# Half-array products chained to alternate, the values' projection behind the first scores, and an order chosen with short queues

## The chip, the cores and the metric

The kernel runs on one core of a Trainium2 chip. The profile names the core's engines: PE multiplies matrices (PEld loads its weights beside it), ACT, DVE and POOL work elementwise, and SP issues the weight transfers. The metric is the time of one execution on the device in microseconds (us), given as the median of several runs. The profile and the trace come from one execution, whose own time stands in the table below.

## The reference

A network of twelve residual sub-layers over 256 tokens of width 1024. Every sub-layer normalizes its input, computes, and is added to the residual stream.

```python
for layer in range(2):                      # first block
    y = even_mixer(...) if layer % 2 == 0 else diff_mixer(...)
    x = x + rms_norm(y, g[1])
    y = memory_cross_attention(rms_norm(x, g[2]), mem_n, ...)
    x = x + rms_norm(y, g[3])
    x = x + rms_norm(swiglu(rms_norm(x, g[4]), ...), g[5])
for l in range(2):                          # second block
    x = x + 0.5 * swiglu_2(rms_norm_2(x, ffn1_norm[l]), ...)
    # neighbourhood attention, gated linear attention (gla), latent attention (mla)
    mixed = gt0 * (y_na @ w_br_na) + gt1 * (y_gla @ w_br_gla) + gt2 * (y_mla @ w_br_mla)
    x = x + mixed @ w_out[l]
    x = x + 0.5 * swiglu_2(rms_norm_2(x, ffn2_norm[l]), ...)
```

`even_mixer` holds two attentions of 8 heads of 64 (`fox_attention`, causal with a bias from forget gates, and `nsa_attention`, the sum of a compressed, a selected and a window branch). `diff_mixer` subtracts one softmax from another. The matrix products of an attention are, for every head,

```python
s = einsum('bqhd,bkhd->bhqk', q, k) * scale      # scores: contraction over the 64 of a head
p = masked_softmax(s, mask)
o = einsum('bhqk,bkhd->bqhd', p, v)              # weighing: 64 results for a query
```

## The kernel before

The twelve stages run in the order even, mem0, ffn0, odd, mem1, ffn1, then f10, mix0, f20, f11, mix1, f21. The 256 tokens are two tiles `t` of 128. Weights are streamed once, in pieces of 512 KB, by the SP queue into four raw buffers (`fetch`, L361). Each piece is split into a high and a low part, the high one by ACT (L386) and the low one by DVE (L388), and a projection adds three products of such parts (L395 to L397, or L403 to L406). Transposes run on PE as well (L451).

The products of attention are in plain f32, and one such product is two instructions in the trace. A head has 64 features, half the height or the width of PE's array of 128 by 128. Scores (`score_unit`, L686) contract over 64 rows: head `h` of a pair uses the row half `h`, and the two halves write to two banks of PSUM, `S[0]` and `S[1]`. A score unit is one tile `t` and two or four pairs of heads; its two banks go through a softmax each (ACT and DVE), are transposed and copied to `PT`, and are then weighed. Weighing (`weigh` L702, and L868 and L872 in `nsa_attention`) has 64 result columns: head `h` uses the column half `h`, and both halves write to one bank `O`. The rotary part of mla (L1311) and the updates and scores of gla (L1397, L1419) work by row halves too. In this text a **piece** is a run of half-array instructions that stand next to each other in PE's order, and the trace writes their shape as `64*128` (row half) or `128*64` (column half).

The order of the instructions on each engine is not the order of the code. The Tile framework's scheduler picks, in a simulation of the time line, what each engine does next, and each engine then runs its list strictly in order. Two things bind the scheduler: data dependences, and `after` (L231), an edge that says that an instruction stands behind another one on its engine. Weights run ahead of their use as far as buffers allow, so projections of the same or the next matrix are there to fill PE while a softmax runs. In `even` and in both halves of `odd` the projection of the values `V` is written ahead of the loop over score units.

At the end of the odd stage the last weighed bank is copied by ACT (`xnA`, L443) and normalized by DVE (`tokA`, L983), then transposed by PE, and the output projection uses it. The same engines split the pieces of the weights that follow, `od_out` and then `memq` of the next stage.

Of the kernel before, what the change touches and what calls it, by code (L numbers as in the profile page):

```python
# [12 lines left out]

F32 = mybir.dt.float32
# [9 lines left out]
KT = 8  # L24
# [177 lines left out]
class Net:  # L202
# [27 lines left out]
    @contextmanager  # L230
    def after(self, *instructions):  # L231

        with ExitStack() as order:
            for i in instructions:
                order.enter_context(self.tc.issue_after(i))
            yield

    def point(self, act, dve):

# [435 lines left out]
    def score_unit(self, unit, qT, kT, extra=None, mask=True):  # L675


        mm = self.nc.tensor.matmul
        t, w, prs = unit
        n = len(prs)  # L680
        S = [self.bank("s")[:, :n * w].rearrange("p (n w) -> p n w", w=w) for _ in range(2)]
        q = slice(t * 128, (t + 1) * 128)
        for i, p in enumerate(prs):
            for h in range(2):
                r = slice(h * 64, h * 64 + 64)
                mm(S[h][:, i], qT[r, p, q], kT(p)[r, :w], start=i == 0 or not mask, stop=not mask)  # L686
        for h in range(2):
            if extra:
                for i in range(0, n, 2):
                    extra(S[h][:, i:i + 2], prs[i] + h, w)  # L690
            if mask:
                mm(S[h][:, :, w - 128:], self.identb, self.causal[:, None, :].to_broadcast([128, n, 128]), start=False,
                   stop=True)
        return S

    def weigh(self, O, V, PTs, prs, nb, c0=0):

        for i, p in enumerate(prs):
            for h in range(2):
                for b in range(nb):  # L700
                    c = c0 + p * 128 + h * 64
                    self.nc.tensor.matmul(O[h * 64:h * 64 + 64, p], V[:, b, c:c + 64], PTs[h][:, i * nb + b], start=b == 0,  # L702
                                          stop=b == nb - 1)


    def rope_consts(self):
# [81 lines left out]
    def even(self, xT, finish, filler):  # L788
        nc = self.nc
        mm = nc.tensor.matmul  # L790
        self.mode("ring")
        st = self.stream("ev_in")
        hd = lambda a: a.rearrange("p (h d) -> p h d", d=64)
        kT, kT2 = self.q4(8), self.u(9)[:, :512].rearrange("p (b n) -> p b n", b=2)

        kk = [self.u(2)[:, t * 416:(t + 1) * 416] for t in range(2)]
        v5 = self.u(1)[:, :768].rearrange("p (t n) -> p t n", t=2)
# [11 lines left out]
        with self.chain():  # L809
# [24 lines left out]
            for t in range(2):  # L834
# [17 lines left out]
                for u in self.causal_units():  # L852
                    if u[0] != t:
                        continue
                    w, prs = u[1:]
                    PTs = [[], []]
                    for br in range(2):
                        for h, S in enumerate(self.score_unit(u, qT2, lambda p: kT2[:, br])):
                            P, r = self.softmax(S)
                            r2 = self.sm(r.shape[-1])  # L860
                            c = 8 + 8 * br + 2 * prs[0] + h
                            nc.vector.tensor_mul(r2, r, gt[:, t, c:c + 2 * len(prs) - 1:2])
                            self.scaled(P, r2)
                            PTs[br].append(self.probsT(self.flat(P)))
                    for i, p in enumerate(prs):
                        for h in range(2):
                            o = O[h * 64:h * 64 + 64, p]
                            mm(o, self.vcbd[:, 2 * p + h], PcT[:, 0], start=True, stop=False)  # L868
                            for br in range(2):
                                for b in range(t + 1):  # L870
                                    c = 128 + br * 128 + h * 64
                                    mm(o, v5[:, b, c:c + 64], PTs[br][h][:, i * (t + 1) + b], start=False,  # L872
                                       stop=br == 1 and b == t)
                s = slice(t * 128, (t + 1) * 128)
                self.split(oT[0][:, 4:8, s], oT[1][:, 4:8, s], O)

# [94 lines left out]
    def odd(self, xT, finish, filler):  # L971
# [14 lines left out]
        for half in range(2):  # L986
# [11 lines left out]
            self.proj(st, xT, KT, (512, lambda t, ps: self.evac(V[:, t], ps)))  # L998
            with self.chain():
                for i, u in enumerate(self.causal_units()):  # L1000
                    t, w, prs = u
                    n = len(prs)
                    S1, S2 = self.score_unit(u, qT, lambda p: kT[:, p])
                    (P1, r1), (P2, r) = self.softmax(S1), self.softmax(S2)
                    r2 = self.sm(n)
                    nc.vector.tensor_scalar(r2, r, self.lamc, None, op0=ALU.mult)
# [292 lines left out]
    def mla(self, qnT, qrT, knT, krT, V):  # L1299
# [3 lines left out]
        for t in range(2):  # L1303
# [5 lines left out]
            for p, h in heads:  # L1309
                r = slice(h * 64, h * 64 + 64)  # L1310
                mm(S[h][:, p], qrT[r, p, tq(t)], krT[r, p], start=False, stop=p == 1)  # L1311
            PTs = self.probs(S)
            for p, h in heads:
                for b in range(2):
# [38 lines left out]
    def gla(self, ls, qk, V, sr, keT):  # L1353
# [20 lines left out]
        for t in range(2):  # L1374
# [5 lines left out]
            for i in range(3):  # L1380
# [9 lines left out]
                else:  # L1390

                    U = [self.bank("o").rearrange("p (h v) -> p h v", h=4) for _ in range(2)]
                    for h in range(4):
                        hs = slice(h * 128, h * 128 + 128)
                        for c in range(2):
                            r = slice(c * 64, c * 64 + 64)
                            mm(U[c][:, h], E[r, hs], V[r, t, hs], start=True, stop=True)  # L1397
# [14 lines left out]
        for t in range(2):  # L1412
            A = self.tile([128, 4, 128], F32, "PT")
            As.append(A)
            parts = [self.bank("s").rearrange("p (h i) -> p h i", h=4) for _ in range(2)]
            for h in range(4):
                for e in range(2):
                    r = slice(e * 64, e * 64 + 64)
                    mm(parts[e][:, h], keT[r, h, tq(t)], qeT[r, h, tq(t)], start=True, stop=True)  # L1419
# [96 lines left out]
        Net(ctx, tc, ins, out).run(stages or STAGES)  # L1516


# [9 lines left out]
```

## Time and profile before

| what | value |
|---|---|
| time, median of 3 runs | 2102.23 us (2100.59 to 2104.03) |
| profiled execution, own time | 2100.82 us |
| span of its trace | 2099.1 us |
| mean granted clock of PE | 0.994 |
| PE busy | 2036.3 us, 97% |
| DVE, ACT, POOL busy | 1389.0, 1168.3 and 88.6 us |

A busy share is time in which an engine's instructions run, and PE's instructions overlap, so the step from one start to the next start is the price of an instruction while nothing waits. In a time line the bracket at the end of a row is idle time before it and what ended that.

### The profile page before, as it was taken

What the parts mean: (1) busy time and instruction counts of PE and PEld (TensorE: products, weight loads), DVE (VectorE), ACT (ScalarE), POOL (GpSimd) and SP (SyncE); (2) the same over time, 40 slices, a digit from 0 to 9 for tenths busy, and PEclk for the clock granted to TensorE, in tenths of its full rate; (3) what the DMA queues carried; (4) which work ended last, traced back from release to release, by engine and by line L of the source; (5) the groups of instructions that cost most, each with busy time, mean ns of one, the idle gap of its engine ahead of it and who ended that gap; (6) DMA issues with size and microseconds to landing.
All of it is one profiled execution on the core that took longest, in us unless ns stands there. A gap on an engine that the chain in (4) does not pass through costs nothing.

```text
span 2099.1 us, 31060 instructions
## 1 busy us (share of the span) xinstructions
PE 2036.3 (97%) x11244; PEld 1707.1 (81%) x11244; DVE 1389.0 (66%) x2878; ACT 1168.3 (56%) x2547; POOL 88.6 (4%) x173
## 2 busy tenths in 40 slices
PE   7998899999799999999999999999999999999999
PEld 6876788877688889887777888888888777879887
DVE  7756765577676657565758777666664667877663
ACT  6645665455566556554654556555654555556652
POOL 1000000000100000001100000000000100100000
PEclk9999999999999999999999999999999999999999
DMA  7505476433457546553443566554653443556750
GB/s 237 176 18 188 161 231 189 145 132 120 161 170 239 184 147 219 196 181 107 148 157 119 168 201 233 190 190 150 227 188 117 149 151 116 181 171 206 235 182 31
DMA packets 100474, 352.16 MB, mean 168 GB/s; under 512 B 12468, under 2 KB 12980, under 8 KB 100320
## 3 DMA queue, kind: packets, MB, share of 16 engines
q1 hardware_dynamic: 96912, 337.99, 49.1%
q0 software_dynamic: 3408, 12.20, 1.9%
q8 instruction: 88, 1.44, 0.3%
q14 instruction: 66, 0.54, 0.1%
HBM read 349.09 MB, written 1.05 MB: 167 GB/s over the span
## 4 chain that ended last, share of the span: by engine, by line
PE 89%; DVE 5%; DMA 2%; ACT 2%; issue 1%; POOL 0%; SPq 0%; ACTq 0%; DVEq 0%; POOLq 0%
PE ps_a L395 10%; PE ps_a L397 10%; PE ps_a L396 10%; PE ps_s L406 8%; PE ps_s L404 5%; PE ps_o L395 4%; PE ps_o L397 4%; PE ps_o L396 4%; PE ps_u L406 4%; PE ps_t L406 4%; PE ps_u L404 2%; PE ps_t L404 2%; PE ps_s L397 2%; PE ps_s L395 2%; PE ps_s L396 2%; PE ps_s L686 2%
## 5 line engine op out<-in xcount | busy, mean ns | idle before, releaser
L388 DVE TENSOR_TENSOR ring<-raw,ring 128x512 fp32r<-128x512 f32 x724 | 467.3, 680 | 179.3 <-ACT ring L386 172.6
L386 ACT ACTIVATE ring<-raw 128x512 fp32r<-128x512 f32 x724 | 411.9, 617 | 189.8 <-PE ps_a L397 64.5
L388 DVE TENSOR_TENSOR slot<-raw,slot 128x512 fp32r<-128x512 f32 x548 | 355.7, 686 | 187.0 <-ACT slot L386 185.1
L386 ACT ACTIVATE slot<-raw 128x512 fp32r<-128x512 f32 x548 | 314.4, 622 | 168.4 <-PE ps_o L397 108.1
L395 PE MATMUL ps_a<-ring,XX 128*128 128x512 f32 (+3 forms) x560 | 216.6, 390 | 6.0 <-ACT XX L386 4.7
L397 PE MATMUL ps_a<-ring,XX 128*128 128x512 f32 (+3 forms) x560 | 216.6, 387 | 0.2 <-DVE XX L388 0.2
L396 PE MATMUL ps_a<-ring,XX 128*128 128x512 f32 (+3 forms) x560 | 214.7, 384 | 0.1
L406 PE MATMUL ps_s<-XX,slot 128*128 128x512 f32 x492 | 178.1, 393 | 0.0
L404 PE MATMUL ps_s<-XX,slot 128*128 128x256 f32 x552 | 145.6, 281 | 0.0
L395 PEld LDWEIGHTS ps_a<-ring,XX 128*128 128x128 f32 x560 | 105.9, 189 | 29.5 <-ACT XX L386 6.7
L397 PEld LDWEIGHTS ps_a<-ring,XX 128*128 128x128 f32 x560 | 105.9, 189 | 23.1 <-issue 3.9
L396 PEld LDWEIGHTS ps_a<-ring,XX 128*128 128x128 f32 x560 | 106.1, 189 | 19.1 <-DVE ring L388 0.8
L404 PEld LDWEIGHTS ps_s<-XX,slot 128*128 128x128 f32 x552 | 103.7, 188 | 6.8
L406 PEld LDWEIGHTS ps_s<-XX,slot 128*128 128x128 f32 x492 | 92.4, 188 | 18.7
L406 PE MATMUL ps_s<-XX,ring 128*128 128x512 f32 x264 | 96.2, 393 | 0.0
L406 PE MATMUL ps_t<-XX,slot 128*128 128x512 f32 x258 | 93.3, 393 | 0.0
L428 POOL TENSOR_TENSOR sm<-sm,mhalf 128x1 f32<-128x1 f32 (+2 forms) x72 | 60.7, 844 | 676.7 <-DVE sm L425 394.6
L395 PE MATMUL ps_s<-slot,XX 128*128 128x256 f32 x288 | 81.9, 285 | 3.8 <-ACT XX L386 3.0
L406 PE MATMUL ps_u<-XX,slot 128*128 128x512 f32 x234 | 84.2, 393 | 0.0
L397 PE MATMUL ps_s<-slot,XX 128*128 128x256 f32 x288 | 81.9, 288 | 0.1
L396 PE MATMUL ps_s<-slot,XX 128*128 128x256 f32 x288 | 81.0, 282 | 0.0
L404 PE MATMUL ps_s<-XX,ring 128*128 128x256 f32 x312 | 79.8, 281 | 0.0
(436 smaller groups left out, 4645.0 us busy)
## 6 DMA issues: line engine op xcount, KB each, us to landing
raw<-f SPq DMA_DIRECT2D x264, 512.0 KB, 4.4
raw<-ffn SPq DMA_DIRECT2D x132, 512.0 KB, 4.3
raw<-win SPq DMA_DIRECT2D x52, 512.0 KB, 4.2
raw<-wgt SPq DMA_DIRECT2D x48, 512.0 KB, 4.1
raw<-od_in SPq DMA_DIRECT2D x24, 512.0 KB, 3.9
raw<-wbr SPq DMA_DIRECT2D x24, 512.0 KB, 4.2
raw<-ev_in SPq DMA_DIRECT2D x16, 512.0 KB, 4.3
raw<-wout SPq DMA_DIRECT2D x16, 512.0 KB, 3.8
```

The costliest lines, as they stand in the source:

```text
L386: a = nc.scalar.activation(hi, src, AF.Copy, scale=scale)
L388: b = nc.vector.tensor_tensor(lo, src, hi.bitcast(F32), op=ALU.subtract)
L395: mm(out, a[0], b[0], start=first, stop=False)
L396: mm(out, a[0], b[1], start=False, stop=False)
L397: mm(out, a[1], b[0], start=False, stop=last)
L404: mm(out[:, :256], w[1], self.XX[:, k, 0], start=False, stop=False)
L406: mm(out, w[0], self.XX[:, k], start=False, stop=last)
L428: self.pow = nc.gpsimd.tensor_tensor(r, v, self.mhalf[:, :n], op=ALU.pow).ins
L686: mm(S[h][:, i], qT[r, p, q], kT(p)[r, :w], start=i == 0 or not mask, stop=not mask)
```

## The change

There are three parts. `burst` issues a list of products with an `after` edge from each to the next, so that they stand in that order on PE, though other instructions may stand between them. Scores, weighing, the rotary part of mla and two loops of gla use it with the halves taken alternately (second half first, except in mla). In `even` and `odd` the projection of `V` is called behind the first score unit's products. And `late_choice` lowers the number of instructions that the scheduler's simulation lets queue at an engine, to 6 for PE and 3 for ACT, DVE and POOL (35 and 12 in the setting before).

```diff
+    def burst(self, products):
+        last = ()
+        for out, a, b, start, stop in products:
+            with self.after(*last):
+                last = (self.nc.tensor.matmul(out, a, b, start=start, stop=stop).ins,)
...
-        for i, p in enumerate(prs):
-            for h in range(2):
-                r = slice(h * 64, h * 64 + 64)
-                mm(S[h][:, i], qT[r, p, q], kT(p)[r, :w], start=i == 0 or not mask, stop=not mask)
+        rows = (slice(0, 64), slice(64, 128))
+        self.burst((S[h][:, i], qT[rows[h], p, q], kT(p)[rows[h], :w], i == 0 or not mask, not mask)
+                   for i, p in enumerate(prs) for h in (1, 0))
...
-    def weigh(self, O, V, PTs, prs, nb, c0=0):
-        for i, p in enumerate(prs):
-            for h in range(2):
-                for b in range(nb):
-                    c = c0 + p * 128 + h * 64
-                    self.nc.tensor.matmul(O[h * 64:h * 64 + 64, p], V[:, b, c:c + 64], PTs[h][:, i * nb + b], start=b == 0,
-                                          stop=b == nb - 1)
+    def weigh(self, O, V, PTs, prs, nb):
+        self.burst((O[h * 64:h * 64 + 64, p], V[:, b, p * 128 + h * 64:p * 128 + h * 64 + 64], PTs[h][:, i * nb + b],
+                    b == 0, b == nb - 1) for i, p in enumerate(prs) for b in range(nb) for h in (1, 0))
...
+                        products += [(o[h], self.vcbd[:, 2 * p + h], PcT[:, 0], True, False) for h in (1, 0)]
+                        for br in range(2):
+                            for b in range(t + 1):
+                                for h in (1, 0):
...
+                    self.burst(products)
...
-        self.proj(st, xT, KT, (512, lambda t, ps: self.evac(V[:, t], ps)))
...
-            for u in self.causal_units():
+            for i, u in enumerate(self.causal_units()):
                 t, w, prs = u
-                PTs = self.probs(self.score_unit(u, qT, lambda p: kT[:, p], bias))
+                S = self.score_unit(u, qT, lambda p: kT[:, p], bias)
+                if i == 0:
+                    self.proj(st, xT, KT, (512, lambda t, ps: self.evac(V[:, t], ps)))
+                PTs = self.probs(S)
...
+            self.burst((S[h][:, p], qrT[rows[h], p, tq(t)], krT[rows[h], p], False, p == 1) for p, h in heads)
...
+    spec.ENG_ISSUE_QUEUE_DEPTH = {**queues, E.PE: 6, E.Activation: 3, E.DVE: 3, E.Pool: 3}
...
-    with tile.TileContext(nc, schedule_with_timeline_sim=True) as tc:
+    with late_choice(), tile.TileContext(nc, schedule_with_timeline_sim=True) as tc:
```

The same edit as in `even` stands in `odd`, and gla's two loops become bursts as mla's does.

The order of SP stays as it was, apart from names, and so does nearly all of POOL's. PE, ACT and DVE are reordered everywhere. Three places show how.

The first is on PE, in the neighbourhood attention of mix0. `ps_o_9963` is the bank that is weighed into, `PT_9989` and `PT_10010` are the transposed probabilities of the two halves, `ps_s_10079` and `ps_s_10080` are the two banks of the next score unit. Before:

```order
L702 MATMUL ps_o_9963<-PT_9989,slot_9604 64x128 x2
L686 MATMUL ps_s_10079<-slot_9608,slot_9604 128x256 x2
L451 MATMUL ps_t_10005<-identf,P_9991 128x128 x4
L702 MATMUL ps_o_9963<-PT_10010,slot_9604 64x128 x2
L702 MATMUL ps_o_9963<-PT_9989,slot_9604 64x128 x2
L702 MATMUL ps_o_9963<-PT_10010,slot_9604 64x128 x2
```

Of the changed kernel:

```order
L244 MATMUL ps_o_9963<-PT_10010,slot_9604 64x128
L244 MATMUL ps_o_9963<-PT_9989,slot_9604 64x128
L244 MATMUL ps_o_9963<-PT_10010,slot_9604 64x128
L244 MATMUL ps_o_9963<-PT_9989,slot_9604 64x128
L244 MATMUL ps_o_9963<-PT_10010,slot_9604 64x128
L244 MATMUL ps_o_9963<-PT_9989,slot_9604 64x128
L244 MATMUL ps_o_9963<-PT_10010,slot_9604 64x128
L244 MATMUL ps_o_9963<-PT_9989,slot_9604 64x128
L244 MATMUL ps_s_10079<-slot_9608,slot_9604 128x256
L459 MATMUL ps_t_10040<-identf,P_10026 128x128 x4
L244 MATMUL ps_s_10080<-slot_9608,slot_9604 128x256
L244 MATMUL ps_s_10079<-slot_9608,slot_9604 128x256
```

The weighing of a unit, which stood in two pieces of one half and then three blocks, is now one piece whose halves alternate, and the score unit's products, which stood two of one half together, are interleaved with the other bank's.

The second is on PE, in a score unit of the window branch in the even stage. `ps_s_887` and `ps_s_886` (before: `ps_s_932`) are its banks, `ps_a_...` is a projection's bank, `causal` is the mask. Before:

```order
L451 MATMUL ps_t_805<-identf,P_789 128x128 x4
L686 MATMUL ps_s_887<-slot_195,slot_191 128x256 x2
L692 LDWEIGHTS identb
L692 MATMUL ps_s_887<-causal,identb 128x2x128
L395 MATMUL ps_a_1699<-ring_1666,slot_199 128x512
L396 MATMUL ps_a_1699<-ring_1666,slot_199 128x512
L397 MATMUL ps_a_1699<-ring_1666,slot_199 128x512
L686 MATMUL ps_s_932<-slot_195,slot_191 128x256 x2
```

Of the changed kernel:

```order
L244 MATMUL ps_s_887<-slot_195,slot_191 128x256
L403 MATMUL ps_a_1450<-ring_1398,XX 128x512
L404 MATMUL ps_a_1450<-ring_1398,XX 128x512
L405 MATMUL ps_a_1450<-ring_1398,XX 128x512
L403 MATMUL ps_a_1450<-ring_1405,XX 128x512
L404 MATMUL ps_a_1450<-ring_1405,XX 128x512
L459 MATMUL ps_t_828<-identf,P_812 128x128 x4
L244 MATMUL ps_s_886<-slot_195,slot_191 128x256
L244 MATMUL ps_s_887<-slot_195,slot_191 128x256
L244 MATMUL ps_s_886<-slot_195,slot_191 128x256
```

A bank that had its two products and its mask in one go now gets its first product alone, with projection products and transposes behind it, and its second one between the products of the other bank.

The third is on ACT, at the end of the odd stage. `xnA_5168` is the copy of the last weighed bank `ps_o_5120`, `raw_5386` is a piece of `od_out`, `raw_5587` and `raw_5594` are pieces of `memq`, the next stage's weights, and `slot_4226` takes the transposed result. Before:

```order
L386 ACTIVATE slot_5388<-raw_5386 128x512 x2
L386 ACTIVATE ring_5589<-raw_5587 128x512 x2
L435 ACTIVATE xn_5444,sm_5443<-ps_a_5393 128x512
L386 ACTIVATE ring_5596<-raw_5594 128x512 x2
L443 ACTIVATE xnA_5168<-ps_o_5120 128x512
L435 ACTIVATE xn_5447,sm_5446<-ps_a_5394 128x512
L386 ACTIVATE slot_4226<-ps_t_5177,subg 128x4x128
```

Of the changed kernel (`raw_5351`, `raw_5365` and `raw_5379` are pieces of `od_out` as well):

```order
L394 ACTIVATE ring_5353<-raw_5351 128x512 x2
L451 ACTIVATE xnA_5168<-ps_o_5120 128x512
L394 ACTIVATE slot_5388<-raw_5386 128x512 x2
L394 ACTIVATE slot_4228<-ps_u_5296 128x512
L394 ACTIVATE ring_5367<-raw_5365 128x512 x2
L394 ACTIVATE ring_5381<-raw_5379 128x512 x2
L394 ACTIVATE ring_5589<-raw_5587 128x512 x2
L394 ACTIVATE slot_4226<-ps_t_5177,subg 128x4x128
```

The copy of the weighed bank stood behind the splits of two pieces of the next stage's weights and now stands five rows ahead of the first of them.

## Rows read from the trace of the kernel before

**Rows 1.** The page, part 1: busy time, share of the span, instructions.

```profile
PE 2036.3 (97%) x11244; PEld 1707.1 (81%) x11244; DVE 1389.0 (66%) x2878; ACT 1168.3 (56%) x2547; POOL 88.6 (4%) x173
```

**Rows 2.** The page, part 4: the chain that ended last, by engine.

```profile
PE 89%; DVE 5%; DMA 2%; ACT 2%; issue 1%; POOL 0%; SPq 0%; ACTq 0%; DVEq 0%; POOLq 0%
```

**Rows 3.** Windows: us, PE, PEld, DVE, ACT, POOL busy, PEclk, DMA, GB/s.

```profile
82.00:135.00 53.00, 53.00 (x321) 39.84 (x320) 33.19 (x98) 23.44 (x83) 0.00 (x0) 1.00 0.18 54
135.00:173.00 38.00, 36.80 (x245) 27.20 (x245) 24.88 (x58) 22.28 (x64) 0.73 (x3) 1.00 0.37 122
187.00:223.00 36.00, 26.49 (x153) 20.16 (x151) 21.24 (x47) 16.51 (x50) 2.86 (x5) 0.86 0.24 84
548.00:552.00 4.00, 2.11 (x7) 1.91 (x8) 3.81 (x7) 0.69 (x1) 0.09 (x1) 0.50 0.26 102
```

**Rows 4.** Groups of PE by line and form: busy, mean ns, idle before.

```profile
L686 PE MATMUL ps_s<-slot,slot 64*128 64x256 f32 x176 | 42.9, 402 | 1.3 <-DVE slot L1074 1.3
L702 PE MATMUL ps_o<-PT,slot 128*64 128x128 f32 x208 | 24.8, 303 | 8.1 <-DVE PT L414 5.0 <-ACT PT L412 3.1
```

**Rows 5.** Time line of PE, 1013 to 1020: start, length, instructions.

```profile
1013.86 1.14 PE L686 MATMUL ps_s<-slot,slot 64*128 64x256 f32 x8
1014.92 0.43 PE L397 MATMUL ps_a<-ring,XX 128*128 128x352 f32 x1
...
1018.67 1.13 PE L686 MATMUL ps_s<-slot,slot 64*128 64x256 f32 x4
1019.73 0.43 PE L395 MATMUL ps_a<-ring,XX 128*128 128x352 f32 x1
```

**Rows 6.** Time line of PE, 1025 to 1030.

```profile
1025.29 0.28 PE L396 MATMUL ps_a<-ring,XX 128*128 128x256 f32 x1
1025.40 0.28 PE L397 MATMUL ps_a<-ring,XX 128*128 128x256 f32 x1
1025.61 0.65 PE L702 MATMUL ps_o<-PT,slot 128*64 128x128 f32 x4
1026.19 1.13 PE L686 MATMUL ps_s<-slot,slot 64*128 64x256 f32 x4
...
1028.69 1.09 PE L702 MATMUL ps_o<-PT,slot 128*64 128x128 f32 x12 [0.78 <-DVE PT L414]
1029.71 0.38 PE L395 MATMUL ps_a<-ring,XX 128*128 128x256 f32 x1
```

**Rows 7.** Time line of ACT, 541 to 546.

```profile
541.37 1.15 ACT L386 ACTIVATE ring<-raw 128x512 fp32r<-128x512 f32 x2 [4.98 <-DMA raw<-memq]
...
544.82 0.58 ACT L443 ACTIVATE xnA<-ps_o 128x512 f32<-128x512 f32 x1
```

**Rows 8.** Time line of DVE at 549.

```profile
549.06 0.69 DVE L983 TENSOR_TENSOR tokA<-ps_o,sm 128x512 f32<-128x512 f32 x1
```

**Rows 9.** Time line of PE, 549 to 561.

```profile
549.89 1.09 PE L451 MATMUL ps_t<-identf,tokA 128*128 128x128 f32 x4 [7.33 <-DVE tokA L983]
550.63 0.78 PE L395 MATMUL ps_o<-ring,slot 128*128 128x512 f32 x1
...
555.04 0.60 PE L451 MATMUL ps_u<-identf,xn 128*128 128x128 f32 x4
...
559.84 0.39 PE L396 MATMUL ps_o<-slot,slot 128*128 128x512 f32 x1
...
560.98 0.29 PE L395 MATMUL ps_a<-ring,XX 128*128 128x256 f32 x1
```

**Rows 10.** Time line of PE, 107 to 132: two score units' banks.

```profile
107.19 1.13 PE L686 MATMUL ps_s<-slot,slot 64*128 64x256 f32 x4
...
110.06 1.13 PE L686 MATMUL ps_s<-slot,slot 64*128 64x256 f32 x4
...
126.82 1.13 PE L686 MATMUL ps_s<-slot,slot 64*128 64x256 f32 x4
...
131.31 0.91 PE L686 MATMUL ps_s<-slot,slot 64*128 64x256 f32 x3
```

More of the change, by code (lines that the diff above doesn't have):

```diff
@@ L11 @@
 from concourse.bass_utils import run_bass_kernel_spmd
+from concourse.hw_specs import get_hw_spec
 from concourse.masks import make_identity
@@ L864, in even @@
                             PTs[br].append(self.probsT(self.flat(P)))
+                    products = []
                     for i, p in enumerate(prs):
[L866 to L870, printed above, removed]
+                        o = [O[h * 64:h * 64 + 64, p] for h in range(2)]
+                        products += [(o[h], self.vcbd[:, 2 * p + h], PcT[:, 0], True, False) for h in (1, 0)]
+                        for br in range(2):
+                            for b in range(t + 1):
+                                for h in (1, 0):
                                     c = 128 + br * 128 + h * 64
-                                    mm(o, v5[:, b, c:c + 64], PTs[br][h][:, i * (t + 1) + b], start=False,
-                                       stop=br == 1 and b == t)
+                                    products.append((o[h], v5[:, b, c:c + 64], PTs[br][h][:, i * (t + 1) + b], False,
+                                                     br == 1 and b == t))
+                    self.burst(products)
                 s = slice(t * 128, (t + 1) * 128)
@@ L997, in odd @@
             self.proj(st, xT, KT, (512, evk), (512, evq), tags=("ao", "a")[half])
-            self.proj(st, xT, KT, (512, lambda t, ps: self.evac(V[:, t], ps)))
             with self.chain():
@@ L1003, in odd @@
                     S1, S2 = self.score_unit(u, qT, lambda p: kT[:, p])
+                    if i == 0:
+                        self.proj(st, xT, KT, (512, lambda t, ps: self.evac(V[:, t], ps)))
                     (P1, r1), (P2, r) = self.softmax(S1), self.softmax(S2)
@@ L1308, in mla @@
                 mm(S[h][:, p], qnT[:, 2 * p + h, tq(t)], knT[:, 2 * p + h], start=p == 0, stop=False)
-            for p, h in heads:
-                r = slice(h * 64, h * 64 + 64)
-                mm(S[h][:, p], qrT[r, p, tq(t)], krT[r, p], start=False, stop=p == 1)
+            rows = (slice(0, 64), slice(64, 128))
+            self.burst((S[h][:, p], qrT[rows[h], p, tq(t)], krT[rows[h], p], False, p == 1) for p, h in heads)
             PTs = self.probs(S)
@@ L1392, in gla @@
                     U = [self.bank("o").rearrange("p (h v) -> p h v", h=4) for _ in range(2)]
[L1393 to L1397, printed above, removed]
+                    heads = [slice(h * 128, h * 128 + 128) for h in range(4)]
+                    self.burst((U[c][:, h], E[r, hs], V[r, t, hs], True, True) for h, hs in enumerate(heads)
+                               for c, r in ((1, b), (0, f)))
                     if t == 0:
@@ L1415, in gla @@
             parts = [self.bank("s").rearrange("p (h i) -> p h i", h=4) for _ in range(2)]
[L1416 to L1419, printed above, removed]
+            self.burst((parts[e][:, h], keT[r, h, tq(t)], qeT[r, h, tq(t)], True, True) for h in range(4)
+                       for e, r in ((1, b), (0, f)))
             tmp = self.tile([128, 4, 128], F32, "tok")
@@ L1516, in build, with late_choice @@
         Net(ctx, tc, ins, out).run(stages or STAGES)
+@contextmanager
+def late_choice():
+    spec = get_hw_spec("TRN2")
+    queues = spec.ENG_ISSUE_QUEUE_DEPTH
+    E = mybir.EngineType
+    spec.ENG_ISSUE_QUEUE_DEPTH = {**queues, E.PE: 6, E.Activation: 3, E.DVE: 3, E.Pool: 3}
+    try:
+        yield
+    finally:
+        spec.ENG_ISSUE_QUEUE_DEPTH = queues
 def kernel(**inputs):
```

## The prediction

> **What bounds the kernel now.** I read the page's busy shares first: PE is busy 2036.3 of 2099.1 us, DVE 1389.0 and ACT 1168.3 [rows 1]. The chain that ended last says the same as a path: 89% PE, and next to nothing but DVE, DMA and ACT, which PE waited for, in the rest [rows 2]. So a microsecond leaves in one of two ways only: PE does the same products in less time, or one of its waits goes. All waits together are 2099.1 - 2036.3 = 62.8 us. The windows tell where: in the even stage's attention PE is idle for 0 and 1.2 us [rows 3], in mem0 for 36.00 - 26.49 = 9.5 us [rows 3]. The time lines then give what half-array products cost beside others [rows 5, 6] and one long stall at the odd stage's end [rows 7 to 9].
>
> **Prices of half-array products.** Twelve weighing instructions, which are six products in the order two, two, two by halves, take 29.71 - 28.69 = 1.02 us; four of one half, two products, take 26.19 - 25.61 = 0.58 [rows 6]. If neighbours of opposite halves run beside each other, the six need four slots and the two need two: two slots more cost 0.44, so a slot of 128 columns is 0.22 (0.215 taken, half of the 0.43 below) and leaving the piece 0.14. The step into the piece is 0.21 where the row before it shows 0.11 for the same form [rows 6], so entering adds 0.1. In the scores, two products of one half take 1.06, and four that alternate take 1.06 too [rows 5]: two slots each. With twice the columns a slot is 0.43, and leaving costs 1.06 - 0.86 = 0.2. A piece thus costs 0.25 by columns and 0.3 by rows on top of its slots.
>
> **Part 1, alternating products.** I counted slots in the instruction orders of both programs: neighbours of opposite halves share one, any other product has its own, and a foreign instruction ends a piece.
> - Column halves, 128 columns (weighing): 173 slots in 47 pieces before, 127 in 28 after: -46 x 0.215 = -9.9, and -19 x 0.25 = -4.7.
> - Row halves, 256 columns (scores and mla's rotary part): 84 in 42 before, 72 in 53 after: -12 x 0.43 = -5.1, and +11 x 0.3 = +3.3. The pieces grow because a burst's first product often stands alone, as the second place in the order shows.
> - Row halves, 128 columns (the smaller scores, gla): 72 in 17 before, 62 in 22 after: -10 x 0.215 = -2.1, +5 x 0.3 = +1.5.
>
> The sum is -9.9 - 4.7 - 5.1 + 3.3 - 2.1 + 1.5 = -17.0 us, of it about -10.4 in even, -2.9 in odd and -3.2 in the two mix stages. All of it is PE's own time on the path, as far as PE does not wait afterwards. The bounds are -12 (the column pieces' exits, -4.7, turn out hidden) and -19 (the lone products' entries are hidden instead, most of +4.8).
>
> A rule bears on the weighing. The six products in one bank took 1.02, four slots [rows 6]. The Trainium skill, TensorEngine Tiling (Array Packing), Restrictions and Gotchas, says of row tiles that different ones cannot access the same PSUM bank at the same time. The weighing's halves are column halves that share one bank; by that rule, carried over to columns, its 46 slots would not be saved, and the sum would be 9.9 less. The trace speaks against that: without overlap the six would be 6 x 0.22 + 0.14 = 1.46.
>
> **Part 2, V behind the first scores.** The same products and the same evacuations are issued; what moves is when the first unit's scores may start and what is left to fill PE behind them. I take 0 for the move by itself: 82 to 135 has no wait that it could remove, 53.00 busy of 53.00 [rows 3]. What hides it is the projections' supply; where this runs dry, the cost is in the term for waits below.
>
> **Part 3, another order everywhere.** The edges of a burst and the queue depths issue nothing. Their price is in which waits go and come.
>
> The one that I can name goes at the odd stage's end. ACT's split of a `memq` piece waited 4.98 us for its DMA and began at 541.37; the copy `xnA` queued behind it began at 544.82 only [rows 7], DVE's `tokA` at 549.06 [rows 8], and PE stood idle 7.33 us until 549.89 [rows 9]. Then the clock stood at 0.50, the lower level of 1.2 GHz, in 548 to 552 [rows 3], after that idle time: twelve products took 555.04 - 550.63 = 4.41, where five such take 560.98 - 559.84 = 1.14 at full clock, so 12 x 0.228 = 2.74 [rows 9], a loss of 1.7. In the new order of ACT `xnA` stands ahead of the `memq` splits, and on PE 27 products of 512 columns and four transposes now stand between this weighing and its transposes: 27 x 0.228 = 6.2 us of cover for the 549.89 - 544.82 = 5.1 from the copy's start to the transposes. I take all of it: -7.33 - 1.7 = -9.0; the bounds are 0 and -9.0. What is late next there is the same `memq` DMA, which nothing but mem1 needs now.
>
> Other waits: the diff touches only orders, so the bounds come from the windows. Above, +12: the 10.4 us that PE saves in even all become idle, beside the 1.2 already there [rows 3]. Below, -4: less than half of mem0's 9.5 idle is filled, since twelve 256-column products (12 x 0.11 = 1.3 us, [rows 6]) and some transposes now stand ahead of its weighing. I take +2, near the even window's 1.2: DVE is busy there for 33.19 + 24.88 = 58.1 of 91 us, and in the 81 that the saving leaves it would be at 72%, a little above its 66% of the whole [rows 1].
>
> **Sum.** 2100.82 - 17.0 - 9.0 + 2 = 2076.8 for an execution like the profiled one; the median stands 1.4 above that one, so 2078.
>
> **Rivals.**
> - Softmax becomes the bound in even (2086). PE has less to do while ACT and DVE do as much, so some 8 of the 10 us saved come back as waits before transposes and weighing. For it: PE already idles 8.1 us ahead of the weighing, all behind evacuations of `PT` [rows 4], and V's projection now fills another place. Against: no idle at all in 82 to 135, where DVE is busy for 63%.
> - The odd stage's end stays (2087). The DMA of `memq` is late by itself, and PE may run out of products where the supply of `od_out` is what lacks; then -9.0 is lost. For it: SP's order is as before, and the wait was on a DMA. Against: the copy no longer stands behind it.
> - Slower: the burst's first product is late (2118). It belongs to half 1 and waits for the bank that comes free last; with every edge behind it, half 0's scores can no longer start early, and PE, strictly in order, holds all that follows. Before, half 0's products ran ahead of half 1's by 110.06 - 107.19 = 2.87 in one unit and 131.31 - 126.82 = 4.49 in another [rows 10], 3.7 on average. In 21 units the halves stood apart. If all of that lead became idle time, it would cost 21 x 3.7 = 77 us; with 2.0 us uncovered in each it is 42, and 2078 + 42 - 2 = 2118. It decides from (2102 - 2076) / 21 = 1.24 us uncovered per unit on. For it: little projection work is left late in even. Against: in the new order projection products stand between the lone first product and the rest, which is the cover.
> - Two column halves of one bank do not overlap (2088): the 46 slots stay, 9.9 us, by the mechanism weighed above with the skill's rule.
> - The change doing nothing is excluded by the orders, which differ as described; better than forecast (2068) is the case in which mem0's and the mix stages' waits are filled as well.
>
> **How the numbers follow.** Forecast 2078: 0.60. Softmax bound 0.14, the odd end stays 0.12, slower 0.05, no overlap 0.03, better 0.06. The forecast's own range is 2070 to 2085, by the bounds of part 1 and half of the other waits' bounds. The range for 8 in 10 goes to 2062 on the side of the better case and to 2096 where both losing cases fall together (2078 + 8 + 9 = 2095). What a measurement of this kernel can tell from no change is about 0.2%, 4.2 us: faster is below 2098.0, which holds all cases but the slower one, less 0.05 for two or three losses adding up: 0.90. Within 0.2%: 0.05. Slower: 0.05.
>
> **What would show it.** Weighing pieces of eight products that last about 1.02 us rather than 1.60, and PE's busy time of the even stage 10 us lower: part 1. No idle of several us ahead of the transposes of `tokA`, and full clock behind them: part 3. Idle time ahead of transposes of `P` in the even window, with PE busy well under DVE's wait: the first rival. Rows of idle ahead of the first score product of a unit: the slower case. I would be wrong as a whole if PE's busy time fell by less than 10 us, or if its idle time, 62.8 now, grew.

## The result, and the profile after

The changed kernel takes 2078.09 us (median of 4 runs, 2076.83 to 2078.74) beside 2103.05 us of the kernel before: a ratio of 0.9882, with a 95% interval of 0.9865 to 0.9899. The forecast was 2078. The total hides a miss on either side, which the stages show. Its trace spans 2077.0 us, 22.1 less than before.

The page of the changed kernel, parts 1 and 4, against [rows 1, 2]:

```profile
PE 2020.6 (97%) x11244; PEld 1691.4 (81%) x11244; DVE 1398.2 (67%) x2878; ACT 1186.0 (57%) x2547; POOL 95.6 (5%) x173
...
PE 83%; DVE 7%; DMA 5%; ACT 3%; issue 1%; POOL 0%; SPq 0%; ACTq 0%; DVEq 0%; POOLq 0%
```

PE is busy 15.7 us less for the same 11244 instructions, and its idle time fell from 62.8 to 56.4: about 70% of the gain is cheaper work, the rest is waits. On the chain DMA has gone from 2% to 5% and DVE from 5% to 7%.

For the stages I add up, in each trace, the steps from one PE product's start to the next one's; the second row prices the order's slots and pieces as the prediction does, and "waits" are what steps take beyond the price that the same step has in the trace of before, where that is over 0.1 us.

| changed minus before, us | even | odd | mem0, mem1 | mix0, mix1 | six ffn stages |
|---|---|---|---|---|---|
| time | -9.3 | -8.8 | +3.9 | -11.3 | +3.4 |
| of it slots and pieces | -10.4 | -2.9 | -0.5 | -3.2 | 0 |
| of it waits | -1.9 | -5.9 | +5.3 | -9.1 | +1.2 |

(What is left, about +5 us in all, lies in the many steps within 0.1 us of their price.) A step that is slow at the lower clock counts as a wait here. Idle time alone, gaps of over 0.15 us put down to the stage of the product that waited, changed by +1.0 in even, -5.2 in odd, +3.2 in mem, -6.6 in mix and +1.0 in ffn. The clock was at its lower level, 0.50 or 1.2 GHz, for 23.9 us before and for 21.5 now.

Groups of PE in the changed kernel by line and form, against [rows 4]:

```profile
L244 PE MATMUL ps_s<-slot,slot 64*128 64x256 f32 x208 | 45.1, 416 | 3.5 <-DVE slot L1084 2.5 <-ACT P L640 1.0
L244 PE MATMUL ps_o<-PT,slot 128*64 128x128 f32 x336 | 25.6, 293 | 2.2 <-DVE PT L422 2.0
...
L244 PE MATMUL ps_s<-slot,slot 64*128 64x128 f32 x144 | 15.8, 292 | 0.0
...
L244 PE MATMUL ps_a<-PT,slot 128*64 128x128 f32 x32 | 2.2, 279 | 1.4 <-ACT PT L420 1.4
```

All weighing in bursts, 368 instructions, now keeps PE busy for 27.8 us. One piece in mix0, on the time line of PE, against [rows 6]:

```profile
1007.74 1.09 PE L244 MATMUL ps_o<-PT,slot 128*64 128x128 f32 x16
1008.76 0.70 PE L244 MATMUL ps_s<-slot,slot 64*128 64x256 f32 x2
```

Eight products take 1.02 us, where [rows 6] had 0.58 and 1.02 for the same eight. The row behind it is a burst's lone first product.

The odd stage's end, on the time lines of ACT, DVE and PE, against [rows 7 to 9]:

```profile
520.13 0.60 ACT L451 ACTIVATE xnA<-ps_o 128x512 f32<-128x512 f32 x1
...
525.18 0.68 DVE L992 TENSOR_TENSOR tokA<-ps_o,sm 128x512 f32<-128x512 f32 x1
...
526.47 0.60 PE L459 MATMUL ps_t<-identf,tokA 128*128 128x128 f32 x4
```

The 7.33 us of idle are gone, and the transposes take 0.60 and not 1.09. The way from the copy's start to the transposes is longer than before (6.3 us, before 5.1); PE has work beside it.

The even windows, against [rows 3]:

```profile
82.00:135.00 53.00, 52.75 (x395) 39.31 (x392) 36.84 (x106) 29.42 (x102) 1.66 (x3) 1.00 0.18 62
135.00:173.00 38.00, 36.58 (x211) 27.83 (x212) 27.37 (x60) 22.51 (x60) 1.74 (x5) 1.00 0.48 165
```

In even PE is idle for 0.25 and 1.42 us: the saved time did not come back as waits there. The waits that grew are in the mem stages (15.7 us of idle time before, 18.9 now), on the time line of PE in the changed kernel:

```profile
206.19 1.09 PE L459 MATMUL ps_t<-identf,P 128*128 128x128 f32 x4 [4.62 <-DVE P L647]
...
568.78 0.63 PE L459 MATMUL ps_t<-identf,P 128*128 128x128 f32 x4 [1.58 <-DVE P L647]
...
571.45 1.09 PE L459 MATMUL ps_t<-identf,P 128*128 128x128 f32 x4 [2.04 <-DVE P L647]
```

PE waits there for a softmax with nothing left to do. Two of the three groups of transposes take 1.09 us, the other one 0.63. The granted clock fell within the first wait (at 205.5); behind it, it is 0.50, the third number from the end of this window:

```profile
206.40:213.00 6.60, 5.37 (x28) 3.91 (x27) 4.54 (x10) 2.17 (x5) 0.65 (x1) 0.50 0.27 79
```

The largest gain in waits is one that the prediction did not name, in the mix stages: 9.3 us of idle time before, 2.7 now. The ends of the two stages hold 4.6 of the 9.3, and 1.0 now. The end of mix0 on PE in the kernel before and in the changed one:

```profile
1225.83 0.50 PE L395 MATMUL ps_a<-ring,slot 128*128 128x512 f32 x1 [0.66 <-ACT slot L386]
...
1228.28 0.66 PE L451 MATMUL ps_u<-identf,slot 128*128 128x128 f32 x4 [1.72 <-DVE slot L390]
```

```profile
1205.43 0.39 PE L405 MATMUL ps_s<-ring,slot 128*128 128x512 f32 x1
1206.44 0.66 PE L459 MATMUL ps_u<-identf,slot 128*128 128x128 f32 x4 [0.62 <-DVE slot L398]
1206.86 0.48 PE L403 MATMUL ps_s<-ring,slot 128*128 128x512 f32 x1
```

Before, the products into `ps_s` that need nothing late had all been done earlier, and PE came to the last transposes with none left. In the changed order they stand around the transposes, and only 0.62 of idle is left.

### The profile page after: what moved, and what is told of

It is laid out like the page before. It is cut to its first block, busy times and chain, and to the rows that moved or that the text cites. A ratio compares the mean times of both kernels' runs of the same rounds, so it can differ in the third digit from the quotient of the medians.

```text
span 2077.0 us, 31127 instructions
## 1 busy us (share of the span) xinstructions
PE 2020.6 (97%) x11244; PEld 1691.4 (81%) x11244; DVE 1398.2 (67%) x2878; ACT 1186.0 (57%) x2547; POOL 95.6 (5%) x173
## 4 chain that ended last, share of the span: by engine, by line
PE 83%; DVE 7%; DMA 5%; ACT 3%; issue 1%; POOL 0%; SPq 0%; ACTq 0%; DVEq 0%; POOLq 0%
PE ps_a L403 10%; PE ps_a L405 10%; PE ps_a L404 10%; PE ps_s L414 8%; PE ps_s L412 5%; PE ps_u L414 4%; PE ps_t L414 4%; PE ps_o L403 4%; PE ps_o L405 4%; PE ps_o L404 4%; PE ps_t L412 2%; PE ps_u L412 2%; PE ps_s L244 2%; DMA raw<-f 2%; DVE ring L396 2%; DMA raw<-ffn 2%
## 5 line engine op out<-in xcount | busy, mean ns | idle before, releaser
L436 POOL TENSOR_TENSOR sm<-sm,mhalf 128x1 f32<-128x1 f32 (+2 forms) x72 | 67.6, 939 | 747.8 <-DVE sm L433 405.9
L576 ACT ACTIVATE half<-ps_s 128x256 f32<-128x256 f32 x108 | 41.3, 382 | 75.7 <-PE ps_s L414 75.6
L403 PE MATMUL ps_s<-slot,XX 128*128 128x256 f32 x288 | 82.3, 287 | 1.4 <-ACT XX L394 1.4
L394 ACT ACTIVATE P<-half 128x256 fp32r<-128x256 f32 x108 | 45.2, 418 | 65.8 <-DVE half L581 65.8
L405 PE MATMUL ps_s<-slot,XX 128*128 128x256 f32 x288 | 81.7, 286 | 0.0
```

What stands on the lines that cost most here:

```text
L394: a = nc.scalar.activation(hi, src, AF.Copy, scale=scale)
L403: mm(out, a[0], b[0], start=first, stop=False)
L405: mm(out, a[1], b[0], start=False, stop=last)
L436: self.pow = nc.gpsimd.tensor_tensor(r, v, self.mhalf[:, :n], op=ALU.pow).ins
L576: nc.scalar.activation(v, ps[:, 256:], AF.Copy)
```

## Experiments

All runs are timed in five rounds beside the kernel before on the same chip; there it took 2105 to 2106 us. Stage columns are as above, against the trace of before, which comes from another chip; a row's stages add up to 1 to 7 us less gain than its ratio (the mean granted clock is 0.994 in that trace and 0.991 to 0.992 in the executions beside the runs). So they show where, and the ratio how much. "Slots" is the price of the order's slots and pieces against before.

| run | ratio (95% interval) | median | slots | even | odd | mem | mix | ffn |
|---|---|---|---|---|---|---|---|---|
| V's move alone | 0.9968 (0.9954, 0.9981) | 2098.48 | -1.1 | +0.4 | -6.5 | +2.3 | -0.1 | +1.0 |
| bursts alone | 0.9931 (0.9917, 0.9944) | 2091.39 | -24.0 | -8.0 | -2.0 | +4.1 | -1.3 | -0.1 |
| bursts and move | 0.9896 (0.9879, 0.9913) | 2083.46 | -23.7 | -7.7 | -10.7 | +3.1 | -3.1 | -0.9 |
| short queues alone | 0.9959 (0.9946, 0.9972) | 2096.76 | +6.0 | -1.9 | -9.1 | +4.4 | -2.4 | +3.3 |
| weighing grouped | 0.9949 (0.9935, 0.9963) | 2094.98 | -1.1 | 0.0 | -8.0 | +6.3 | -7.2 | +3.9 |
| scores grouped | 0.9921 (0.9906, 0.9936) | 2089.47 | -6.1 | -8.1 | -3.3 | +7.4 | -9.0 | +2.0 |
| PE 6, others 12 | 0.9896 (0.9881, 0.9910) | 2084.31 | -18.3 | -9.0 | -7.5 | +8.0 | -11.8 | +5.2 |
| PE 12, others 4 | 0.9839 (0.9825, 0.9853) | 2072.73 | -22.4 | -9.5 | -6.8 | +0.9 | -14.9 | +1.7 |
| control: the changed kernel | 0.9887 (0.9871, 0.9903) | 2080.27 | -16.9 | -10.6 | -6.9 | +4.9 | -12.7 | +2.8 |
| without V's move | 0.9867 (0.9854, 0.9881) | 2077.18 | -16.3 | -9.1 | -10.9 | +5.0 | -13.7 | +4.2 |
| PE 12, others 12 | 0.9838 (0.9824, 0.9851) | 2070.60 | -22.7 | -11.0 | -8.4 | +1.4 | -16.1 | +2.0 |
| bursts and PE 12 alone | 0.9831 (0.9814, 0.9848) | 2069.34 | -22.7 | -10.2 | -9.4 | +4.3 | -16.2 | +0.2 |

**The parts by themselves.** V's move on the kernel before:

```diff
-        self.proj(st, xT, KT, (512, lambda t, ps: self.evac(V[:, t], ps)))
+                S = self.score_unit(u, qT, lambda p: kT[:, p], bias)
+                if i == 0:
+                    self.proj(st, xT, KT, (512, lambda t, ps: self.evac(V[:, t], ps)))
```

> The kernel before with the move of V's projection alone; bursts and queue depths as before. Theory A (time follows the half-array slots, plus the stall at the odd stage's end, which exists if and only if the copy xnA stands behind memq splits on ACT): slots give -1.1 us; in this order xnA stands ahead of both memq splits and 44 rows stand between the last weighing and its transposes on PE, so the stall of 9.0 goes too: 2103 - 10 = 2093. Theory B (the short queues make the gain, by better choices everywhere): no change, 2103 within 2. In the trace A wants idle ahead of the transposes of tokA below 1 us, B wants it above 5.

Measured -6.7 us by the ratio, all of it in odd. Its time lines of ACT and PE:

```profile
532.89 0.57 ACT L443 ACTIVATE xnA<-ps_o 128x512 f32<-128x512 f32 x1
...
536.27 1.15 ACT L386 ACTIVATE ring<-raw 128x512 fp32r<-128x512 f32 x2 [1.11 <-DMA raw<-memq]
...
542.19 0.60 PE L451 MATMUL ps_t<-identf,tokA 128*128 128x128 f32 x4
```

The stall is gone with the queues as they were. Theory B's "no change" falls; A's size was 3 us too large.

The bursts on the kernel before: `burst` and its callers as in the change, and nothing else.

> The kernel before with the bursts alone; V's projection and queue depths as before. Slots: column halves 128 in 30 pieces, 256-column row halves 66 in 44, 128-column row halves 57 in 17, which the prices of the prediction make -24.0 us against the kernel before, more than the -17.0 of the whole change. The copy xnA stands behind both memq splits and only 6 rows stand between the last weighing and its transposes, so the odd end's stall of 9 us stays. Theory A: 2103 - 24 = 2079, to 2083 with some new waits. Theory B (short queues make the gain; the slots saved turn into waits): 2095 or more.

Measured -14.5 us (0.0069 x 2106): neither A's -20 to -24 nor B's -8 at most. ACT and PE at the odd end:

```profile
529.83 1.16 ACT L394 ACTIVATE ring<-raw 128x512 fp32r<-128x512 f32 x2 [4.23 <-DMA raw<-memq]
533.70 1.15 ACT L394 ACTIVATE ring<-raw 128x512 fp32r<-128x512 f32 x2 [2.15 <-DMA raw<-memq]
534.76 0.58 ACT L451 ACTIVATE xnA<-ps_o 128x512 f32<-128x512 f32 x1
...
539.83 1.09 PE L459 MATMUL ps_t<-identf,tokA 128*128 128x128 f32 x4 [8.32 <-DVE tokA L990]
```

The stall stayed, as its order said it would. The slots make 24.0 us and 14.5 reached the time, so 9.5 came back. In the trace, the mix steps beyond their price took back 7.1 of their 8 us and the mem steps 7.4. Little of that is idle time in mix: 10.4 us there, 9.3 before. Most of the rest is the clock. At the end of mix0 PE was idle for 1.11 us and, two products later, for 1.89 (0.66 and 1.72 before). In the second wait the granted clock fell to 0.50 for 6.8 us, and a product of 512 columns took 0.43 us to the next start instead of 0.23. The end of mix1 looks the same, and the trace of before has full clock at both places. The window at mix0:

```profile
1216.80:1223.60 6.80, 5.96 (x16) 4.88 (x17) 3.79 (x7) 1.27 (x3) 0.00 (x0) 0.50 0.88 307
```

In the whole trace the lower clock lasts for 49.1 us, against 23.9 in the trace of before. Over all executions on that chip the difference is smaller: the mean granted clock is 0.9892 with the bursts and 0.9914 before, which would make some 4.6 of the 9.5 us, an estimate from these figures.

One of the new waits is the slower rival's own, a head product that holds PE:

```profile
1019.31 0.70 PE L244 MATMUL ps_s<-slot,slot 64*128 64x256 f32 x2 [1.19 <-DVE sm L435]
```

Bursts and V's move, with the queues of before:

```diff
-    with late_choice(), tile.TileContext(nc, schedule_with_timeline_sim=True) as tc:
+    with tile.TileContext(nc, schedule_with_timeline_sim=True) as tc:
```

> The changed kernel with the scheduler's queue depths as they were before (35 and 12), bursts and V's move kept. Slots -23.7 us against the kernel before (the changed kernel has -16.9), and xnA stands ahead of the memq splits with 44 rows of cover, so -9.0 as well. Theory A: 2103 - 33 = 2070, to 2075 with new waits, faster than the changed kernel's 2078, that is the short queues cost 3 to 8 us. Theory B: 2095 or more, since the short queues make the gain.

Measured -21.9: the sum of the two runs above (-6.7 - 14.5 = -21.2). The two act in different places. The mix end still waits, more than before:

```profile
1204.65 0.50 PE L403 MATMUL ps_a<-ring,slot 128*128 128x512 f32 x1 [1.01 <-ACT slot L394]
...
1207.26 1.12 PE L459 MATMUL ps_u<-identf,slot 128*128 128x128 f32 x4 [1.88 <-DVE slot L398]
```

Short queues on the kernel before: `late_choice` alone.

> The kernel before with the short queues (6, 3) alone. Slots +6.0 us (58 pieces of 256-column row halves instead of 42). xnA stands behind one memq split instead of two, with 23 rows between the last weighing and its transposes, so some 4 of the 9 us may go. Theory A: 2103 + 6 - 4 = 2105, between 2100 and 2109. Theory B: 2085 or less, most of the gain. In the trace of the changed kernel PE's waits in the two mix stages fell by about 9 us together; if the short queues did that, it is seen here too, and 2105 becomes 2096.

Measured -8.6, between the theories and outside A's interval, but near the 2096 (-7) that the expectation gave for the case that the mix waits fall. The stall at the odd end is gone here too, whole and not in part, and waits in the mix stages fell by 7.1, while the order cost 6.0 more in slots. So the short queues do two opposite things: they keep ready products back as cover, and they cut pieces apart. Theory B falls by all four runs, theory A lacked the waits. Theory C puts it together: a part saves what its slots cost as long as PE has ready work left at the next late result, and PE's queue depth decides that. Up to here this is argued; the runs below try it.

**Does alternation itself pay?** The changed kernel, with the halves one after the other in the weighing:

```diff
-                    b == 0, b == nb - 1) for i, p in enumerate(prs) for b in range(nb) for h in (1, 0))
+                    b == 0, b == nb - 1) for h in (1, 0) for i, p in enumerate(prs) for b in range(nb))
...
-                    self.burst(products)
+                    self.burst(products[::2] + products[1::2])
```

> The changed kernel, but the weighing's bursts (the nsa ones too) take all products of half 1 and then all of half 0, instead of alternating; scores, V's move and short queues are kept. The order then has 200 slots of column halves in 27 pieces where the changed kernel has 127 in 28: +73 x 0.215, all other counts within 2 slots, together +15.8 us by the prediction's prices. Theory C (neighbours of opposite column halves run beside each other though they share a bank, and the saved slots reach the end): 0.9882 + 15.8/2103 = 0.9957 of the kernel before, between 0.992 (half hidden in waits) and 0.997. Theory D (they do not overlap, and the gain came from placing the pieces elsewhere): 0.988, within 0.002. The trace settles it too: an eight-product piece lasts 0.215 x 7 + 0.14 = 1.6 us by C and as long as the alternating one by D.

Measured 0.9949, +0.0067 or 14 us above the changed kernel: theory C. The same piece and the weighing's groups in this run:

```profile
1022.67 1.58 PE L244 MATMUL ps_o<-PT,slot 128*64 128x128 f32 x16
1024.18 0.70 PE L244 MATMUL ps_s<-slot,slot 64*128 64x256 f32 x2
```

```profile
L244 PE MATMUL ps_o<-PT,slot 128*64 128x128 f32 x336 | 38.2, 293 | 2.0 <-DVE PT L422 2.0
...
L244 PE MATMUL ps_a<-PT,slot 128*64 128x128 f32 x32 | 3.2, 279 | 0.3 <-ACT PT L420 0.2
```

1.51 us instead of 1.02 for the same sixteen instructions, and 41.4 instead of 27.8 us in all: 13.6 for 73 slots, 0.19 a slot. Column halves that write one bank do run beside each other.

The same for the scores, `for h in (1, 0) for i, p in enumerate(prs)`:

> The changed kernel, but the scores' bursts take all products of half 1 and then those of half 0; weighing, V's move and short queues are kept. Slots of 256 columns 93 in 54 pieces (changed kernel: 72 in 53), of 128 columns 75 in 21 (62 in 22): +10.8 us by the prices. Theory C: 0.9882 + 0.0051 = 0.9933 of the kernel before. Rival: with half 1's bank complete before half 0's first product, its softmax starts one or two slots (0.4 to 0.9 us) earlier in each of some 26 units, and what waits for it gains as much as the slots cost: 0.988, within 0.002.

Measured 0.9921, +0.0039 or 8 us: C's direction, somewhat less than its size; the rival's 0.988 is outside the interval. The 64x256 scores keep PE busy 8.3 us longer and the 64x128 ones 2.2:

```profile
L244 PE MATMUL ps_s<-slot,slot 64*128 64x256 f32 x208 | 53.4, 415 | 2.5 <-DVE slot L1084 2.5
...
L244 PE MATMUL ps_s<-slot,slot 64*128 64x128 f32 x144 | 18.0, 290 | 0.0
```

**Which queue, and how deep?** PE 6 and the others at 12 again:

> The changed kernel with PE's queue of 6, but 12 for ACT, DVE and POOL as before. Slots -18.3 us against the kernel before (changed kernel -16.9), and the end of the mix stages reads as in the changed kernel (transposes three rows behind the first of the last ready products). Theory C, in which it is PE's depth that keeps ready projection products back as cover for late transposes: 0.988 of the kernel before, within 0.002, and waits in each mix stage of about 3.5 us as in the changed kernel. Rival: the short queues of ACT and DVE matter as well (what they split early, and what they evacuate late): 0.9896 or more, as with deep queues, and mix waits of 8 us or more.

0.9896, with an interval that overlaps the ranges of both theories: inconclusive by the time. The waits in mix are as in the changed kernel (-9.6 against -9.1), which is C's; the mem and ffn stages are slower.

PE 12 and the others 4:

> The changed kernel with queues of 12 for PE and 4 for the others. Pieces stay together better: slots -22.4 us against the kernel before (changed kernel -16.9; deep queues -23.7). At the end of the mix stages ten ready products stand between what the late transposes wait for and the transposes, so a part of the cover remains. Theory C: 0.9882 - 5.5/2103 = 0.9856 if the waits stay as in the changed kernel, 0.988 if half of the 5.5 comes back as waits in mix and mem: a value between is expected, 0.987. Rival (slots do not decide, the short queue's choices do): between the changed kernel and the deep queues, 0.989.

0.9839: better than expected by any theory, 9 us below the changed kernel and clear of it by the intervals. The slots come back (-22.4) and the mix waits stay away (-9.3 against -9.1).

The control:

> The changed kernel as it is, as the control for the runs beside it on the same chip. Any theory: 0.988 of the kernel before, within 0.0015, and about 9 us slower than the kernel with queues of 12 and 4 (0.9839).

0.9887, as expected. Its stages differ by up to 2 us from those of the first trace of the same kernel; smaller differences in the table mean nothing.

PE 12 and the others at 12, to settle what the run with 6 left open:

> The changed kernel with PE's queue of 12 and 12 for ACT, DVE and POOL as before (only PE's depth changed from the built-in 35). Slots -22.7 us against the kernel before, as with 12 and 4 (-22.4). Theory C, in which PE's depth decides: 0.984 of the kernel before, within 0.0015, as with 12 and 4. Rival (short queues of the other engines matter, as the 0.9896 against 0.9882 with PE's 6 hints without settling it): 0.9855 or more, the 3 us that were seen there, and then the difference lies in waits of mem0, ffn0, mem1 and ffn1, where those 3 us lay.

0.9838, the same as with 4: with PE at 12 the depths of ACT, DVE and POOL make no difference that can be measured. Bursts and move with PE at 35 took 0.9896, and PE's depth is all that differs between that run and this one. The mix stages tell short from deep in every trace: 9.2 to 10.4 us of idle time in the four with 35, 0.7 to 3.7 in the ten with 6 or 12. At the mix end of this run the last transposes wait for nothing:

```profile
1203.51 0.60 PE L459 MATMUL ps_u<-identf,slot 128*128 128x128 f32 x4
```

**Is V's move needed?** The changed kernel without it:

> The changed kernel with V's projection back ahead of the loop; bursts and short queues (6, 3) kept. Slots -16.3 us against the kernel before (changed kernel -16.9). On ACT the copy xnA stands behind one memq split, on PE 23 rows stand between the last weighing and its transposes. Theory C, with the addition that either the move or the short queues takes the stall at the odd stage's end (the runs with one of them alone both did): 0.9882 + 0.6/2103, and at most 2 us of idle ahead of the transposes, that is 0.9885 to 0.9895. Rival (the move is what takes it; behind a memq split the stall is back whatever the queue): +6 to +9 us, 0.991 to 0.9925.

0.9867, not slower than the control: the rival falls, and even the 2 us of idle did not come. ACT and PE at the odd end of this run, with the last weighing ahead of the transposes:

```profile
529.62 1.15 ACT L394 ACTIVATE ring<-raw 128x512 fp32r<-128x512 f32 x2 [1.16 <-DMA raw<-memq]
530.68 0.58 ACT L451 ACTIVATE xnA<-ps_o 128x512 f32<-128x512 f32 x1
...
528.22 1.06 PE L1031 MATMUL ps_o<-slot,PT 128*128 128x128 f32 x8
...
534.28 0.66 PE L459 MATMUL ps_t<-identf,tokA 128*128 128x128 f32 x4
```

The copy does stand behind a `memq` split that waits for its DMA, and PE loses nothing, since it has 22 products to do meanwhile. So one split ahead of the copy does not bring the stall back. In the kernel before, the last weighing on PE and the second of the two splits on ACT are these:

```profile
540.35 1.06 PE L1024 MATMUL ps_o<-slot,PT 128*128 128x128 f32 x8
...
543.77 1.15 ACT L386 ACTIVATE ring<-raw 128x512 fp32r<-128x512 f32 x2 [0.67 <-DMA raw<-memq]
```

From the weighing's end to the transposes it is 549.89 - 541.41 = 8.5 us, here 534.28 - 529.28 = 5.0; behind it stand 5 products, here 22. By these rows the shorter way is worth some 3.5 us of the 7.33 and the 17 products more, at 0.228 each, some 3.9: an estimate. No run separates the two. Both kernels with the stall have two `memq` splits ahead of the copy and 5 products of cover, all others one split at most and 18 products or more.

The bursts with PE's queue of 12 and nothing else:

```diff
+    spec.ENG_ISSUE_QUEUE_DEPTH = {**queues, E.PE: 12}
```

> The kernel before with the bursts and PE's queue of 12 alone: no move of V's projection, 12 for the other engines as before. Slots -22.7 us against the kernel before, as with the move (0.9838). The copy xnA stands behind one memq split and 19 rows of PE stand between the last weighing and its transposes (19 x 0.228 = 4.3 us of cover; 33 rows with the move). Theory C: the move is not needed, 0.982 to 0.985. Rival (with a cover of 19 rows the stall at the odd stage's end comes back in part): 0.986 to 0.988, and several us of idle ahead of the transposes of tokA.

0.9831 with an interval of 0.9814 to 0.9848, the lowest of all, level with the two other kernels of depth 12 and clear of both the kernel before and the changed one. A cover of 18 products was enough, behind one split. No run has PE's depth of 12 without the bursts, so what the depth gives by itself is open.

## Why the prediction was right, point by point

- **Alternating products, -17.0.** The mechanism is shown by grouping the halves again, which gives back 14 and 8 us. By the steps on PE the column halves gave -14.3 (48.3 to 34.0; forecast -14.6), the 128-column row halves -2.3 (forecast -0.6), and the 256-column row halves +2.2 where -1.8 was forecast. Together that is -14.4. Such a step holds the idle time behind a product as well, and mem0's wait of 4.62 us, shown above, stands behind a score piece. Without idle time the three are -12.4, -1.7 and -2.7, together -16.8: the sum was right. A slot cost 0.19 when grouped, not 0.215.
- **V's move, 0 by itself.** Wrong as a reason, harmless in the sum: on the kernel before the move alone removes the odd end's stall, worth 6.7 us. In the changed kernel it is not needed, since the short queues remove the stall too.
- **The odd end, -9.0.** The stall went whole, the stage gained 8.8 of which 2.9 are slots, so waits gave -5.9. The prediction named two reasons, the copy's new place on ACT and the cover of 27 products. The place is not needed in full: with the copy behind one `memq` split there is no stall either, if PE has cover. How much each of the two gave no run shows; the estimate above has them about equal. The `memq` wait of 4.98 us ended as the last weighing did (541.37 and 541.41); what held the copy from there to 544.82 was the two splits, the row between them and 0.67 us of wait for the second piece.
- **Other waits, +2, bounds -4 and +12.** The net was -4.5 by the steps (all waits -10.4, of it -5.9 in odd), just outside the lower bound, and -1.2 by idle time alone (-6.4, of it -5.2 in odd), inside it; +2 was too high by both. By the steps it is -9.1 in the mix stages, which the prediction did not look at, -1.9 in even, +5.3 in mem, +1.2 in ffn. The small steps took 5 of that back. So the trace's -22.1 is -16.9 by slots at their price, -5.9, -4.5 and +5.2, where the forecast had -17.0, -9.0 and +2: the total is right, and apart from the slots no part is right to better than 3 us. That the misses cancel is luck.
- **Rivals.** Softmax as the bound in even did not come true: idle time there rose by 1.0 of the 10 us saved. Savings came back elsewhere: with the bursts alone 9.5 us of the 24.0, in the mix and mem stages and in part by the lower clock, and in the changed kernel in the mem stages. The odd end stayed only in the run with bursts alone. The slower case exists, 1.19 us at one head product, but all idle in front of scores is 3.5 us, where 26 would have been needed. Column halves in one bank overlap, as the grouped weighing shows, so the rival that carried the rule of the Trainium skill (TensorEngine Tiling (Array Packing), Restrictions and Gotchas) over to them falls; for row halves in one bank no run here shows it, since they write two.

What stays open: what makes the mem stages slower, by 0.9 to 8.0 us in every run of the table, with PE's depth at 6, 12 and 35 alike. No run took one mem wait away by itself.

## What to carry to other kernels

Products that fill half of PE's array should stand next to a product of the other half: on this chip sixteen instructions took 1.02 us alternating and 1.51 grouped. A saving on the busiest engine only reaches the end where independent work is still left to fill the next wait, so count the ready products behind a late result before counting the saving. An idle stretch can cost twice, once as idle time and once by the lower clock behind it: in the trace of the bursts alone the clock was at 0.50 for 49.1 us, 23.9 before. When a scheduler's look-ahead is tuned, read both what it keeps back as cover and what it cuts apart: here 35 was too deep and 6 too shallow for PE, and the bursts with 12 beat the whole change by 0.5% of the time.

## What the runs showed of the hardware beyond that

A single 256-column product of one half costs as much as two of opposite halves: in mix0 of the changed kernel a lone one took 1009.39 - 1008.76 = 0.63 us to the next start, and a pair 1004.36 - 1003.72 = 0.64.

```profile
1003.72 0.70 PE L244 MATMUL ps_s<-slot,slot 64*128 64x256 f32 x4
1004.36 0.43 PE L403 MATMUL ps_a<-ring,XX 128*128 128x352 f32 x1
...
1009.39 0.66 PE L459 MATMUL ps_t<-identf,P 128*128 128x128 f32 x4
```
